# Narrower moving operands in the sums of squares, and more filler products at the head, in a one-layer decoder block

## Chip, cores and metric

The kernel runs on one core of a Trainium2 chip. The time is the device time of one execution in microseconds (us). A core has a matrix engine (TensorE, in the profile PE, its weight loads PEld), a vector engine (VectorE, DVE), an engine for activation functions (ScalarE, ACT), a general one (GpSimd, POOL) and queues for transfers (SP's queue carries nearly all of them here).

## What is computed

One layer over 512 tokens of 1024 features, all float32: two gated feed-forward parts with a token-mixing part between them, each behind an RMSNorm whose result is scaled and shifted by values from a conditioning vector; a last RMSNorm at the end.

```python
def rmsnorm(x, g):
    xf = x.astype(jnp.float32)
    y = xf * lax.rsqrt(jnp.mean(xf * xf, axis=-1, keepdims=True) + EPS)
    return (y * g.astype(jnp.float32)).astype(x.dtype)
...
def reference(x, c, positions, w_ada, b_ada, g_norm_ffn1, w_ffn1_in, ...):
    cos, sin = rope_tables(positions, x.dtype)
    cond = jax.nn.silu(c)
    h = x
    for l in range(DEPTH):
        mod = cond @ w_ada[l] + b_ada[l]
        sh1, sc1, gt1, sh2, sc2, gt2, sh3, sc3, gt3 = [
            m[:, None, :] for m in jnp.split(mod, N_MOD, axis=-1)]
        u = modulate(rmsnorm(h, g_norm_ffn1[l]), sh1, sc1)
        h = h + 0.5 * gt1 * swiglu(u, w_ffn1_in[l], w_ffn1_out[l])
        u = modulate(rmsnorm(h, g_norm_mix[l]), sh2, sc2)
        h = h + gt2 * token_mixing(u, cos, sin, w_in[l], ...)
        u = modulate(rmsnorm(h, g_norm_ffn2[l]), sh3, sc3)
        h = h + 0.5 * gt3 * swiglu(u, w_ffn2_in[l], w_ffn2_out[l])
    return rmsnorm(h, g_final)
```

What matters for the change is the mean of squares over the 1024 features, which every one of the four RMSNorms needs for each token.

## The kernel before

**Layout.** Features lie on the 128 partitions, tokens along the free dimension: the running state is eight tiles H[0] to H[7] of 128 features by 512 tokens. A sum over features is therefore a sum over partitions and over the eight tiles. The tiles' squares are first added up elementwise (on VectorE); the sum over the 128 partitions is then a matrix product. The stationary operand is a 128x128 piece of the squares (features by tokens), the moving operand a 128x128 tile of ones (`self.ones`), so that the output has tokens on partitions, with the same sum in each of its 128 columns. One column per piece is read (`bank[:, ::P]`) by the square root, whose result goes to `r4`: four columns, one for each 128 tokens. A reciprocal on VectorE follows. Then `spread` (line 460; in the head line 1678) makes from r4 a tile in which every partition has the factors of all tokens, by a product whose stationary operand is a column of r4 broadcast and whose moving operand is the identity.

**The stream.** The weights arrive by transfer on SP's queue, are split into a high part (line 317, ScalarE) and a low part (line 329, VectorE), and each product of the large matrices is three passes (lines 360 to 362, 747 to 749, and in the head 1718, 1720, 1722). Nothing reorders the work: each engine runs its instructions in the order in which the code writes them.

**Where the sums of squares are.** `stats_t` (line 442) is called five times in the middle of the stream and once at the end: in `out_tail` for the first half of the tokens and in `head` for the second half, both of them twice (before token mixing, before the second feed-forward part), in `out_end` for the first half, and for the second half when the last product is over. That last call sums three tiles (`acc`, `s6`, `s`) instead of one, and `s`, the square of the last tile, is ready last. Two filler products (line 625) and the spread stand behind it.

**The head.** `startup` (line 1617) begins with five filler products on ones (line 1630). Transfers bring H in four pieces. ScalarE's silu of the conditioning vector is spread over the partitions by two products of 512 columns (line 1649) and copied by VectorE (line 1652). Then the squares of H[0] to H[7] follow one by one on ScalarE (line 1662). Those of H[0] and H[1] are summed over partitions by themselves; from then on VectorE adds two neighbours (line 1666), and the function `part` (line 1655, its products on line 1657) adds the pair's sums into bank 7: four products for a pair. Behind the pairs (2,3) and (4,5) stands one filler product (line 1669, made by `warm`, line 1624), behind the last pair and the square root (line 1670) two (line 1671). VectorE meanwhile works through the conditioning's dot products (`ada_do`, line 387), between whose halves the reciprocal is put (line 1675). The spread (line 1678), five fillers (line 1679), the scaling of tile 0 (line 467 on VectorE, line 479 on ScalarE) and the first pass of the main products (line 1718) follow in this order. Fillers write bank 5 and are read by nobody.

Of the kernel before, what the change touches and what calls it, by code (L numbers as in the profile page):

```python
# [14 lines left out]
P = 128  # L15
T = 512
HT = 256
D = 1024
KT = 8
DFF = 2816  # L20
# [26 lines left out]
def _fmajor(w, cols):  # L47
    k = w.shape[0] // P
    return w[:, cols].reshape(k, P, len(cols)).transpose(1, 0, 2).reshape(P, -1)


def _tiles(*starts):
    return [np.arange(s, s + P) for s in starts]


def _blocks(w, c0, c1, j):

    rows = (w[:D // 2], w[D // 2:])
    return [np.concatenate([_fmajor(rows[i], x) for x in _tiles(c + j * P, c + j * P + P)], axis=1)
# [80 lines left out]
def chunk_widths():  # L140
    outs = [D] * (KT // 2 * (len(PARTS) - 1)) + [(FT - PARTS[-1][0]) * P] * KT
    f1 = [2 * FIRST * P] * KT + [D] * (2 * (FT - FIRST)), outs
    mix = [D] * 24 + [4 * P] * 2 + ([D] * 4 + [4 * P] * 2) * (KT // 2 - 1) + [D] * KT
    return f1, mix, ([D] * (2 * FT), outs)


class Kernel:
# [6 lines left out]
    def plan(self):  # L154
# [21 lines left out]
        def blocks(recs):  # L176
# [5 lines left out]
            for need, src, make in ((0, r11, None), (1, x0, (x0, r12, r11)), (2, x1, (x1, r22, x0)), (3, r21, None),  # L182
                                    (3, r12, (r12, r22, r12)), (3, r22, None), (3, x0, (x0, r21, x1))):
                for j, x in enumerate((r11, r12, r22, r21)):
                    if x == src or (make and x in make):
                        self.last[n + j] = len(self.order)
                self.order.append((D, n + need, src, make))

# [175 lines left out]
    def settle(self, bank, hi, uh):  # L364

        self.nc.tensor.matmul(bank[:, :HT - SHIFT], hi, uh[:, SHIFT:HT], start=True, stop=True, skip_group_check=True)

# [74 lines left out]
    def stats_t(self, bank, hs, parts=None, between=None):  # L442


        n = (hs.stop - hs.start) // P
        r, c = self.r4[:, hs.start // P:hs.stop // P], slice(hs.start, hs.stop, P)
        parts = parts or (self.acc[:, hs],)
        for j, x in enumerate(parts):
            for i in range(n):
                self.nc.tensor.matmul(bank[:, hs.start + i * P:hs.start + i * P + P], x[:, i * P:i * P + P], self.ones,  # L450
                                      start=i == j == 0, stop=j == len(parts) - 1, skip_group_check=True)
        self.nc.scalar.activation(r, bank[:, c], AF.Sqrt, bias=self.eps, scale=1.0 / D)
        if between:
            between()
        self.nc.vector.reciprocal(r, r)
# [20 lines left out]
    def norm_u(self, n, k, hs, t, rest=True):  # L476
# [5 lines left out]
        if n == 2 and hs.start:  # L482
            u = self.U4[1][k // 4]
            act(u[:, k % 4 * HT:(k % 4 + 1) * HT], t[:, hs], AF.Identity, bias=S, scale=1.0)

# [33 lines left out]
    def out_tail(self, ms, ksrc, gate, nxt, squares):  # L519
# [3 lines left out]
        tiles, starts, put = {}, {}, []  # L523
        A, Bh = slice(0, HT), slice(HT, T)
        step = None
        self.held = self.pos
        for h, hs in enumerate((A, Bh)):
            for m in ms:
# [12 lines left out]
                for i, (hi, lo, uh, ul) in enumerate(ks):  # L541
# [6 lines left out]
                    self.mm3(bank[:, hs], hi, lo, uh[:, hs], ul[:, hs], i == 0, i == len(ks) - 1)  # L548
                s = squares(m)[:, :HT]
                self.tail_step(m, hs, bank, gate, s)  # L550
# [13 lines left out]
    def out_end(self, ms, ksrc, gate):  # L564
# [3 lines left out]
        tiles = {}  # L568
        A, Bh = slice(0, HT), slice(HT, T)
        rA, rB = self.B[6], self.B[7]  # L570
# [12 lines left out]
        for h, hs in enumerate((A, Bh)):  # L583
            for m in ms:
# [9 lines left out]
                for i, (hi, lo, uh, ul) in enumerate(tiles[m]):  # L594
# [9 lines left out]
                    self.mm3(bank[:, hs], hi, lo, uh[:, hs], ul[:, hs], i == 0, i == n - 1)  # L604
                s = self.tp.tile([P, T], F32, name="ut")[:, :HT]
                self.tail_step(m, hs, bank, gate, s)
# [1010 lines left out]
    def startup(self):  # L1617
        nc, a = self.nc, self.a
        v, M = nc.vector, nc.tensor.matmul


        def warm(n, x):
            for _ in range(n):
                M(self.B[5][:, :P], self.ones, x[:, :P], start=True, stop=True)


        nc.scalar.dma_start(self.cond[0:1, :], a["c"])
        nc.scalar.preload_act_table(AF.Silu)
        v.memset(self.ones, 1.0)
        warm(5, self.ones)  # L1630

        row = self.X[0]
        v.memset(row, 0.0)
        v.memset(self.eps, EPS)
        v.memset(self.hpi, float(np.pi / 2))
        for k in range(0, KT, 2):
            two = slice(k * T, (k + 2) * T)
            nc.sync.dma_start(self.Hall[:, two], a["xT"][:, two])
        self.ada_fetch(0)
        nc.sync.dma_start(self.vecs, a["vecs"])  # L1640
        self.ada_fetch(8, 2)
        nc.sync.dma_start(self.cst, a["cst"][:, :163])
        self.fetch(0)
        self.ada_fetch(1)
        self.ada_fetch(9)
        self.fetch(1)
        nc.scalar.activation(row[0:1, :], self.cond[0:1, :], AF.Silu)
        for i in range(2):
            M(self.B[i], self.ones, row[:, i * T:(i + 1) * T], start=True, stop=True)
        nc.scalar.preload_act_table(AF.Sqrt)  # L1650
        for i in range(2):
            v.tensor_copy(self.cond[:, i * T:(i + 1) * T], self.B[i])


        def part(s, first, last):
            for n in range(4):
                M(self.B[7][:, n * P:(n + 1) * P], s[:, n * P:(n + 1) * P], self.ones, start=first and n == 0, stop=last,
                  skip_group_check=True)

        s = [self.acc, self.R] + [self.Xall[:, i * T:(i + 1) * T] for i in range(2, KT)]  # L1660
        for k in range(KT):
            nc.scalar.activation(s[k], self.H[k], AF.Square)
            if k < 2:
                part(s[k], not k, False)
            elif k % 2:
                v.tensor_tensor(s[k - 1], s[k - 1], s[k], op=OP.add)
                part(s[k - 1], False, k == KT - 1)
                if k + 1 < KT:
                    warm(1, self.H[k])
        nc.scalar.activation(self.r4, self.B[7][:, ::P], AF.Sqrt, bias=self.eps, scale=1.0 / D)  # L1670
        warm(2, self.H[7])

        g, b1 = self.g(0), self.vecs[:, 8:16]
        self.ada_do(0)
        self.ada_do(8, 2, lambda: v.reciprocal(self.r4, self.r4))

        for n in range(4):
            M(self.B[6][:, n * P:(n + 1) * P], self.r4[:, n:n + 1].to_broadcast([P, P]), self.ident, start=True, stop=True)
        warm(5, self.H[7])
        v.scalar_tensor_tensor(b1, b1, 1.0, g, op0=OP.add, op1=OP.mult)  # L1680
        self.ada_fin("shift", 0, 1)

        def scale(k):
            m = self.mod[:, 8 + k:9 + k]
            v.scalar_tensor_tensor(m, m, g[:, k:k + 1], b1[:, k:k + 1], op0=OP.mult, op1=OP.add)

        scale(0)
        banks = list(self.B)
        full = slice(0, T)
        self.Rn = {0: self.B[6]}  # L1690
        self.split_hi()
        t = self.norm_t(0, 0, full)
        self.norm_u(0, 0, full, t, rest=False)
        self.ada_do(1)
        self.norm_b(0, 0, full, t)
        self.split_lo()
        nc.scalar.activation(self.R, self.B[6], AF.Copy)
        self.Rn[0] = self.R
        self.norm_x(0, full, t)
        for k in range(KT):  # L1700
            if k + 1 < KT:
                if k:
                    self.ada_do(k + 1)
                self.ada_fin("shift", k + 1, k + 2)
                self.ada_do(9 + k)
                scale(k + 1)
                t = self.norm_t(0, k + 1, full)
            self.split(k + 1)
            if k + 1 < KT:
                self.norm_u(0, k + 1, full, t)  # L1710
                self.norm_b(0, k + 1, full, t)
            if k + 2 < KT:
                self.ada_fetch(k + 2)
                self.ada_fetch(10 + k)
            self.fetch(k + 2)
            w = self.take()
            for (hi, lo), b in zip(w, banks):
                M(b, hi, self.UH[k], start=k == 0, stop=False)  # L1718
            for (hi, lo), b in zip(w, banks):
                M(b, hi, self.UL[k], start=False, stop=False)  # L1720
            for (hi, lo), b in zip(w, banks):
                M(b, lo, self.UH[k], start=False, stop=k == KT - 1)  # L1722
        self.ada_next = self.ada_ahead = 16
        self.ada_stop = 24
        self.bg_fetch()
        adds, self.splits = self.u_steps(0)
        for f in adds:
            f()
        for j in range(FIRST):
            self.split(self.pos + j)  # L1730
            self.fetch()
            self.ffn_post(j, self.ffn_silu(j, banks[2 * j]), banks[2 * j + 1])
# [59 lines left out]
```

## Time and profile before

| | |
|---|---|
| three runs | 991.28, 990.26, 991.11 us; median 991.11 |
| the profiled execution | 990.14 us, of which the span from the first to the last instruction is 988.4 us |
| TensorE busy | 980.2 us, 99% of the span, 6688 multiplications |
| VectorE, ScalarE busy | 783.5 us, 475.2 us |
| sums of squares, line 450 | 32 instructions, 348.4 to 981.0 us |
| sums of squares in the head, line 1657 | 40 instructions, 6.0 to 11.6 us |
| fillers of the head, line 1624 | 28 instructions, 1.0 to 14.6 us |

A float32 product is two instructions on TensorE, each with its own weight load. A row of the view in order of time has the start, the stretch that it covers, the engine, the line, the operation, output<-inputs, the shape and the count, and in brackets the idle time ahead of it and what ended it. A shape such as 128*64 128x256 has the stationary operand first (128 rows by 64 columns) and the moving one behind it (128 partitions by 256 columns). A row of a line's instructions has their durations as minimum/median/maximum in ns. A row of a group has its busy time in us and, behind the comma, the mean of one in ns. A row of TensorE's waits has the total in us, how often, and the longest. A row by stretch has the length, the busy time of PE, PEld, DVE, ACT and POOL with their instruction counts, the granted clock of TensorE, the share of the transfer engines and GB/s.

### The profile page before, as it was taken

How to read it: one execution, taken by the hardware profiler on the slowest of the kernel's cores; microseconds unless marked ns; L12 is line 12 of the kernel's file. 1: busy time of each engine (PE TensorE's matmuls, PEld its weight loads, DVE VectorE, ACT ScalarE, POOL GpSimd, SP SyncE). 2: the span in 40 equal slices, each digit the busy share in tenths (PEclk: the TensorE clock that was granted, in tenths of full speed). 3: DMA queues.
4: the chain of work that ended last, by engine and by line, in shares of the span. 5: the costliest groups of instructions: out<-in, count | busy, mean ns of one | idle time of the engine just before them, and what ended most of it. 6: DMA issues, size and time to landing. Idle time of an engine off the chain costs nothing.

```text
span 988.4 us, 16359 instructions
## 1 busy us (share of the span) xinstructions
PE 980.2 (99%) x6688; PEld 892.8 (90%) x6688; DVE 783.5 (79%) x1089; ACT 475.2 (48%) x713; POOL 29.7 (3%) x31
## 2 busy tenths in 40 slices
PE   9999999999999999999999999999999999999997
PEld 7888998989999899788879998998899898998997
DVE  7989979889797677888879877768787777676764
ACT  6453643625435453446545553455355254352553
POOL 0000000000000000006200000000000000000002
PEclk9999999999999999999999999999999999999999
DMA  9856445464563416654233326513344134241312
GB/s 348 279 191 230 150 149 186 157 195 164 181 204 110 138 57 200 224 184 160 67 125 110 107 74 221 172 47 103 103 153 133 47 119 135 86 150 44 108 42 86
DMA packets 44876, 141.74 MB, mean 143 GB/s; under 512 B 6273, under 2 KB 9089, under 8 KB 44802
## 3 DMA queue, kind: packets, MB, share of 16 engines
q1 hardware_dynamic: 44224, 140.18, 43.7%
q8 instruction: 52, 0.85, 0.4%
q10 hardware_dynamic: 578, 0.53, 0.2%
q14 instruction: 22, 0.18, 0.1%
HBM read 135.29 MB, written 2.24 MB: 139 GB/s over the span
## 4 chain that ended last, share of the span: by engine, by line
PE 94%; DVE 2%; SPq 1%; DMA 1%; issue 1%; ACT 0%; POOL 0%; POOLq 0%; DVEq 0%; ACTq 0%
PE bank L360 15%; PE bank L361 15%; PE bank L362 15%; PE bank L748 13%; PE bank L747 13%; PE bank L749 13%; PE bank L1718 2%; PE bank L1722 1%; PE bank L1720 1%; SPq L1055 1%; PE bank L1101 1%; PE bank L1399 1%; PE bank L1152 1%; PE bank L1400 1%; PE bank L1401 1%
## 5 line engine op out<-in xcount | busy, mean ns | idle before, releaser
L329 DVE TENSOR_TENSOR wlo<-raw,whi 128x1024 fp32r<-128x1024 f32 (+4 forms) x162 | 170.4, 1064 | 52.5 <-ACT whi L317 52.2
L747 PE MATMUL bank<-UH,whi 128*128 128x256 f32 x640 | 176.7, 276 | 0.0
L748 PE MATMUL bank<-UL,whi 128*128 128x256 f32 x640 | 176.7, 276 | 0.0
L749 PE MATMUL bank<-UH,wlo 128*128 128x256 f32 x640 | 176.7, 276 | 0.0
L317 ACT ACTIVATE whi<-raw 128x1024 fp32r<-128x1024 f32 (+4 forms) x162 | 146.3, 921 | 58.6 <-DVE raw L261 55.1
L360 PE MATMUL bank<-HI,whi 128*128 128x512 f32 (+1 forms) x406 | 146.2, 360 | 0.0
L361 PE MATMUL bank<-HK,whi 128*128 128x512 f32 (+1 forms) x406 | 145.9, 359 | 0.0
L362 PE MATMUL bank<-HI,wlo 128*128 128x512 f32 (+1 forms) x406 | 145.8, 359 | 0.0
L329 DVE TENSOR_TENSOR wlo<-X,whi 128x1024 fp32r<-128x1024 f32 (+3 forms) x104 | 111.8, 1083 | 30.9 <-ACT whi L317 30.5
L747 PEld LDWEIGHTS bank<-UH,whi 128*128 128x128 f32 x640 | 120.1, 188 | 0.4
L748 PEld LDWEIGHTS bank<-UL,whi 128*128 128x128 f32 x640 | 120.2, 188 | 0.0
L749 PEld LDWEIGHTS bank<-UH,wlo 128*128 128x128 f32 x640 | 120.1, 188 | 0.0
L747 PE MATMUL bank<-SH,whi 128*128 128x256 f32 x408 | 112.6, 276 | 0.0
L748 PE MATMUL bank<-SL,whi 128*128 128x256 f32 x408 | 112.6, 276 | 0.0
L749 PE MATMUL bank<-SH,wlo 128*128 128x256 f32 x408 | 112.6, 276 | 0.0
L317 ACT ACTIVATE whi<-X 128x1024 fp32r<-128x1024 f32 (+3 forms) x104 | 95.7, 943 | 34.1 <-DVE X L261 33.4
L360 PE MATMUL bank<-UH,whi 128*128 128x512 f32 (+1 forms) x304 | 105.7, 348 | 0.0
L361 PE MATMUL bank<-UL,whi 128*128 128x512 f32 (+1 forms) x304 | 104.3, 343 | 0.1
L362 PE MATMUL bank<-UH,wlo 128*128 128x512 f32 (+1 forms) x304 | 104.1, 342 | 0.0
L362 PEld LDWEIGHTS bank<-HI,wlo 128*128 128x128 f32 x406 | 76.2, 188 | 11.7
L360 PEld LDWEIGHTS bank<-HI,whi 128*128 128x128 f32 x406 | 76.2, 188 | 11.5
L361 PEld LDWEIGHTS bank<-HK,whi 128*128 128x128 f32 x406 | 76.3, 188 | 11.3
(344 smaller groups left out, 1837.3 us busy)
## 6 DMA issues: line engine op xcount, KB each, us to landing
raw<-wmix SPq DMA_DIRECT2D x44, 512.0 KB, 3.8
raw<-wf1i SPq DMA_DIRECT2D x31, 512.0 KB, 4.9
raw<-wf2i SPq DMA_DIRECT2D x30, 512.0 KB, 3.7
ada<-wada SPq DMA_DIRECT2D x23, 512.0 KB, 5.6
AR<-wada SPq DMA_DIRECT2D x19, 512.0 KB, 4.5
X<-wf2i SPq DMA_DIRECT2D x14, 512.0 KB, 3.6
cs<-wada SPq DMA_DIRECT2D x12, 512.0 KB, 3.7
X<-wf1i SPq DMA_DIRECT2D x12, 512.0 KB, 4.3
```

Source lines behind the costliest of these rows:

```text
L317: self.nc.scalar.activation(self.hi[:, y], r[:, x], AF.Copy)
L329: self.nc.vector.tensor_tensor(self.lo[:, y], r[:, x], self.hi[:, y], op=OP.subtract)
L360: M(ps, hi, uh, start=start, stop=False)
L361: M(ps, hi, ul, start=False, stop=False)
L362: M(ps, lo, uh, start=False, stop=stop)
L747: M(o, hi, uh, start=start and p == 0 and k == 0, stop=False, skip_group_check=True)
L748: M(o, hi, ul, start=False, stop=False, skip_group_check=True)
L749: M(o, lo, uh, start=False, stop=k == 3, skip_group_check=True)
L1055: nc.sync.dma_start(w[32 * o:32 * o + 32], t[32 * i:32 * i + 32])
L1101: nc.tensor.matmul(S[:, o], q[:, toks], k[:, ks], start=True, stop=True, skip_group_check=True)
L1152: self.nc.tensor.matmul(self.bO[64 * h:64 * h + 64, P * hp:P * hp + P], x, pt[:, (2 * h + j) * P:(2 * h + j + 1) * P], start=j == first, s ...
L1718: M(b, hi, self.UH[k], start=k == 0, stop=False)
```

## The change

The moving operand of every sum of squares becomes 16 columns of ones instead of 128, and so does the output of each; the column that the square root reads is the first of them. In the head, the fillers behind the pairs (2,3) and (4,5) become three products instead of one, and those behind the square root four instead of two.

```diff
+NARROW = 16
...
         for j, x in enumerate(parts):
             for i in range(n):
-                self.nc.tensor.matmul(bank[:, hs.start + i * P:hs.start + i * P + P], x[:, i * P:i * P + P], self.ones,
+                t = hs.start + i * P
+                self.nc.tensor.matmul(bank[:, t:t + NARROW], x[:, i * P:i * P + P], self.ones[:, :NARROW],
                                       start=i == j == 0, stop=j == len(parts) - 1, skip_group_check=True)
...
         def part(s, first, last):
             for n in range(4):
-                M(self.B[7][:, n * P:(n + 1) * P], s[:, n * P:(n + 1) * P], self.ones, start=first and n == 0, stop=last,
-                  skip_group_check=True)
+                M(self.B[7][:, n * P:n * P + NARROW], s[:, n * P:(n + 1) * P], self.ones[:, :NARROW],
+                  start=first and n == 0, stop=last, skip_group_check=True)
...
                 if k + 1 < KT:
-                    warm(1, self.H[k])
+                    warm(3, self.H[k])
         nc.scalar.activation(self.r4, self.B[7][:, ::P], AF.Sqrt, bias=self.eps, scale=1.0 / D)
-        warm(2, self.H[7])
+        warm(4, self.H[7])
```

## The prediction

> **What bounds the kernel now.** I read the page first, then the list of TensorE's waits, then the two lines that the change touches, then the head in order of time.
>
> ```profile
> span 988.4 us, 16359 instructions
> PE 980.2 (99%) x6688; PEld 892.8 (90%) x6688; DVE 783.5 (79%) x1089; ACT 475.2 (48%) x713; POOL 29.7 (3%) x31
> ...
> PE 94%; DVE 2%; SPq 1%; DMA 1%; issue 1%; ACT 0%; POOL 0%; POOLq 0%; DVEq 0%; ACTq 0%
> ```
>
> TensorE is busy for 99% of the span and owns 94% of the chain that ended last. Its waits on other engines, over the whole run, are these five:
>
> ```profile
> PE bank L1624 <- DVE ones L1629: 1.1, 1, 1.1
> PE bank L1718 <- ACT UH L479: 0.5, 1, 0.5
> PE bank L460 <- DVE r L455: 0.3, 1, 0.3
> PE bank L1678 <- DVE r L1675: 0.2, 1, 0.2
> PE bank L450 <- ACT ut L517: 0.2, 1, 0.2
> ```
>
> Together 2.3 us. So a TensorE instruction saved in the stream is time saved, a late start of the main stream at line 1718 has hardly any later wait to hide in, and the change can matter in three places: the head, the five sums inside the stream, and the sum at the very end.
>
> **The price of a sum of 16 columns.** Each float32 product is two instruction pairs, a weight load and a multiplication.
>
> ```profile
> L450 PE MATMUL bank<-ones,AR x24: 270/274/275, 348.4 to 979.7; 128*128 128x128 f32 x24
> ```
>
> The change leaves the weights (128x128 squares) as they are and shortens only what moves past them. The question is which of the two sets the pace. Loads:
>
> ```profile
> L1187 PEld LDWEIGHTS bank<-cst,f x8: 85/88/90, 502.3 to 502.9; 128*8 128x8 f32 x8
> L1152 PEld LDWEIGHTS bank<-probT,v x120: 132/137/137, 405.3 to 494.6; 128*64 128x64 f32 x120
> L450 PEld LDWEIGHTS bank<-ones,AR x24: 187/191/192, 348.3 to 979.5; 128*128 128x128 f32 x24
> 9.44 0.19 PEld L1657 LDWEIGHTS bank<-ones,X 128*128 128x128 f32 x1
> 9.44 0.30 PEld L1657 LDWEIGHTS bank<-ones,X 128*128 128x128 f32 x2
> 470.53 0.97 PEld L1101 LDWEIGHTS bank<-k,q 64*128 64x128 f32 x16 [0.17 <-issue]
> 501.25 0.21 PEld L1245 LDWEIGHTS bank<-k,wpool 64*64 64x64 f32 x8 [0.35 <-issue]
> ```
>
> 8, 64 and 128 columns take 88, 137 and 191 ns: (191-88)/120 = 0.86 ns a column over a fixed part, so 128 columns keep the load path 110 ns. The two rows at 9.44 say the same: after a pause of TensorE the first load runs 0.19 us, two end after 0.30, so the second begins 0.30-0.19 = 0.11 us behind the first, before any multiplication could have held it back. Today's pace is 0.111 us a pair ((0.97-0.19)/7 in the rows of eight loads below). Load and multiplication therefore cost the same today, and shortening one leaves the other. **I take 0.111 us a pair: nothing saved in the stream.** The other end is the 16 loads at line 1101, (0.97-0.19)/15 = 0.052 us each; there they alternate between two halves of the array's rows, which these do not. Farther off, line 1245's eight loads go to different quarters, (0.21-0.13)/7 = 0.011 us, the 0.13 us being (by the slope above) what one of 64 columns takes. Full-height loads of 128 columns are nearest the first two rows. A dearer pair than today's I exclude: the load is unchanged and the multiplication shorter.
>
> What does get shorter is the end of the last multiplication:
>
> ```profile
> L747 PE MATMUL bank<-UH,whi 128*128 128x256 f32 x640 | 176.7, 276 | 0.0
> L361 PE MATMUL bank<-HK,whi 128*128 128x512 f32 x298 | 116.0, 389 | 0.0
> ```
>
> 256 more columns are 113 ns, 0.44 ns a column; a float32 row of 128 columns lasts as long as 256 of these (275 at most against 276), so 112 columns fewer end 112 x 0.88 = 0.10 us sooner.
>
> [...]
>
> **The head, step by step.** Lines 1657 (sums), 1624 (fillers), 1666 (adds of squares).
>
> ```profile
> 6.46 1.75 PEld L1657 LDWEIGHTS bank<-ones,AR 128*128 128x128 f32 x15 [0.24 <-issue]
> 8.13 0.97 PEld L1657 LDWEIGHTS bank<-ones,X 128*128 128x128 f32 x8
> 8.70 0.69 DVE L1666 TENSOR_TENSOR X<-X 128x512 f32<-128x512 f32 x1 [0.75 <-ACT X L1662]
> 9.03 0.30 PEld L1624 LDWEIGHTS bank<-H,ones 128*128 128x128 f32 x2
> 9.44 0.97 PEld L1657 LDWEIGHTS bank<-ones,X 128*128 128x128 f32 x8
> 9.98 0.69 DVE L1666 TENSOR_TENSOR X<-X 128x512 f32<-128x512 f32 x1 [0.59 <-ACT X L1662]
> 10.33 0.30 PEld L1624 LDWEIGHTS bank<-H,ones 128*128 128x128 f32 x2
> 10.73 0.97 PEld L1657 LDWEIGHTS bank<-ones,X 128*128 128x128 f32 x8
> 11.61 0.53 PEld L1624 LDWEIGHTS bank<-H,ones 128*128 128x128 f32 x4
> 11.92 0.26 ACT L1670 ACTIVATE r<-bank,eps 128x4 f32<-128x4 f32 x1 [1.98 <-PE bank L1657]
> 12.35 0.17 DVE L1675 RECIPROCAL r<-r 128x4 f32<-128x4 f32 x1
> 12.57 0.97 PEld L1678 LDWEIGHTS bank<-cst,r 128*128 128x128 f32 x8 [0.43 <-DVE r L1675]
> 15.33 2.11 PE L1718 MATMUL bank<-UH,whi 128*128 128x512 f32 x8 [0.48 <-ACT UH L479]
> 20.87 1.67 PEld L1718 LDWEIGHTS bank<-UH,whi 128*128 128x128 f32 x8 [0.24 <-ACT UH L479]
> ```
>
> Today the last two sums start when their adds end (8.70+0.69 = 9.39, then 9.44; 9.98+0.69 = 10.67, then 10.73), and the fillers fill most of the gaps, which leave 0.19, 0.18 and, ahead of line 1678, 0.52 us. The change puts four more pairs (0.44 us) into each. With 0.111 us a pair: sums at 8.13 to 9.02, six filler pairs to 9.69, sums to 10.58, six to 11.24, sums to 12.13 (11.61 today, 0.52 later), eight filler pairs to 13.02. The bank is complete 0.52-0.10 = 0.42 us later, so the root (line 1670) runs from 12.34 to 12.60. Today the reciprocal does not wait for it (12.18 to 12.35 is VectorE's own order); then it will, starts about 12.63, 0.28 us late, and behind it wait VectorE's second half of line 387, lines 390, 1680, 400 and 1685. Line 1678 could follow at 12.85, but the fillers ahead of it in TensorE's order hold it to 13.02: **0.45 us late**. Line 467 waits for its products, line 479 for that, and the main stream for line 479: from 15.33 to 15.78. The second round (20.87) waits for the same engines, behind the same delay, so nothing is won back there. Bounds: with a pair of 0.052 us the narrow sums end before their adds and the fillers fit in; the head is then no later, nor earlier, since the reciprocal keeps its place in VectorE's order. Thus 0 to +0.45; I take +0.45.
>
> **The stream and the end.** Five calls of line 450 (two in out_tail, two in head, one in out_end) have four pairs each, 20 pairs at an unchanged 0.111: 0. Bounds: at 0.052, 20 x 0.059 = 1.2 us saved.
>
> ```profile
> 980.10 0.42 ACT L517 ACTIVATE ut<-H 128x256 f32<-128x256 f32 x1 [0.46 <-DVE H L516]
> 980.56 0.52 PEld L450 LDWEIGHTS bank<-ones,ut 128*128 128x128 f32 x4 [0.38 <-ACT ut L517]
> 981.31 0.26 ACT L452 ACTIVATE r<-bank,eps 128x2 f32<-128x2 f32 x1 [0.80 <-PE bank L450]
> 981.83 0.97 PEld L460 LDWEIGHTS bank<-cst,r 128*128 128x128 f32 x8 [0.30 <-DVE r L455]
> ```
>
> At the end only the four pairs behind the last square (980.10+0.42) are exposed; the eight ahead of them lie in that wait. The last multiplication ends 0.10 us sooner, the root, the reciprocal, line 460 and the stores follow: -0.10. At 0.052 a pair, three steps more, -0.18: -0.28.
>
> **Sum:** +0.45 + 0 - 0.10 = +0.35 us. The profiled execution took 990.14 us around its span of 988.4; the median of the three runs, 991.11, is 0.97 above it, and their spread is 1.02 us. The profile would be 990.5, the median **991.5 us**.
>
> **Rivals.** One: *half price*. Narrow loads overlap as at line 1101: 0 - 1.2 - 0.28 = -1.5 us, 989.6. For it: that row. Against it: its two row halves, and the two loads at 9.44.
>
> Two, the other side: *the clock falls in the head*.
>
> ```profile
> L1624 PE MATMUL bank<-ones x10: 421/421/579, 1.1 to 3.1; 128*128 128x128 f32 x10
> 6.03 0.59 PE L1649 MATMUL bank<-X,ones 128*128 128x512 f32 x1
> 984.50:985.00 0.50, 0.00 (x0) 0.00 (x0) 0.15 (x1) 0.00 (x0) 0.39 (x1) 1.00 1.01 338
> 985.00:986.00 1.00, 0.00 (x0) 0.00 (x0) 0.00 (x0) 0.00 (x0) 0.00 (x0) 0.63 1.01 339
> ```
>
> TensorE starts slow: 421 ns for what later takes 275. By 6.03 it is fast (512 columns in 0.59 us, more work than those 421 ns). So it took up to 5.0 us from the first product at 1.05. At the other end the granted clock (the third number from the end) is 1.00 to 985 and means 0.63 in the next microsecond, so it halves at 985.26. The last products ran from 981.83 to about 983.0: 1.2 of the last 3.4 us, 34%, did not hold it. After the change, if only moving columns count, the stretch from 6.46 to 9.69 holds 24 narrow pairs of 16 x 0.88 = 14 ns and six fillers of 0.11: 1.0 of 3.2 us, 31%. That is the point: below about 34% by moving columns the clock would halve near 9.7. Up to 5.0 us at half speed lose 2.5 us of products, with the +0.35 a total of +2.9: 994.0. Against it: if loads count as work, the stretch is full. The end's case also had 2.3 us of complete silence. [...]
>
> Three: *the loads hide entirely*, 0.011 us a pair as at line 1245: 20 x 0.10 + 3 x 0.10 + 0.10 = -2.4 us, 988.7. Against it stands everything at 128 full columns.
>
> Four: *the head's delay is swallowed* by a later wait, leaving -0.10, 991.0. The five waits leave 0.5 us for it at most, and those at 1718 come before or with the delay.
>
> **How the numbers follow.** My forecast 0.52; half price 0.14; clock 0.21; hidden loads 0.05; swallowed 0.08. A measurement of this kernel can tell about 0.2%, 2.0 us, from no change. Beyond that lie rival two above and rival three below; from half price (1.5 us) a little falls outside with the runs' 1 us spread, and from the forecast as little above. Faster 0.08, same 0.69, slower 0.23. The range goes from half price less some spread, 989.4, to the clock's 994.0; outside it lie most of rival three and about half of rival two.
>
> **What would show it.** Right: line 1657 and 450 loads still 0.11 us apart, their multiplications about 0.18 us long; line 1675 near 12.6, line 1678 near 13.0, line 1718 near 15.8; the last root near 0.10 us sooner behind the last square. Wrong: pairs of 0.06 us or less; fillers at line 1624 after 9 us lasting 421 ns; line 1718 still at 15.3.

## The result and the profile after

| | kernel before | changed kernel |
|---|---|---|
| runs | 22, median 990.32 us (989.95 to 991.28) | 22, median 995.05 us (990.25 to 995.72) |
| profiled execution | 990.14 us, span 988.4 | 995.06 us, span 993.3 |
| ratio | | 1.0033, 95% interval 1.0022 to 1.0044 |

The change made the kernel slower. The ratio, 0.33%, is an average over two sorts of runs: of the 22, fifteen took 994.68 to 995.72 us and seven 990.25 to 990.88, with nothing between them. The runs of before form one group. So the usual loss is 995.05 - 990.32 = 4.7 us, and in a third of the runs there is none. The granted clock of the whole execution tells the same two sorts apart: it is 0.993 to 0.995 in each of the fifteen, and 0.998 to 1.000 in each of the seven, as in the runs of the kernel before.

The profile of the changed kernel is one of the fifteen. Its page, the lines that answer to those of before:

```profile
span 993.3 us, 16383 instructions
...
PE 985.6 (99%) x6700; PEld 898.8 (90%) x6700; DVE 783.4 (79%) x1089; ACT 474.9 (48%) x713; POOL 29.7 (3%) x31
...
PEclk7999999999999999999999999999999999999999
...
PE 95%; DVE 2%; SPq 1%; issue 1%; ACT 1%; POOL 0%; DMA 0%; POOLq 0%; ACTq 0%; DVEq 0%
```

Twelve more instruction pairs, as the added fillers give; every other engine as before; and a first slice of TensorE's clock at 7 tenths, where the kernel before has 9. The same by stretch (length, busy time of PE, PEld, DVE, ACT and POOL with counts, the granted clock, the transfers' share, GB/s):

```profile
6.02:9.43 3.41, 3.41 (x27) 2.96 (x26) 2.38 (x4) 2.81 (x6) 0.00 (x0) 1.00 1.01 393
9.43:19.67 10.24, 10.24 (x49) 10.24 (x49) 4.59 (x15) 1.94 (x6) 0.00 (x0) 0.50 1.02 369
...
19.67:22.00 2.33, 2.31 (x14) 1.86 (x13) 2.33 (x5) 2.33 (x4) 0.00 (x0) 1.00 0.66 193
```

The clock was halved for 10.24 us, beginning 3.41 us after it had first become full at 6.02. (That moment is the first entry of the clock in the trace. Ahead of it the rows by stretch print 1.00 all the same, but the products of line 1627 last 421 ns there and their loads 333 ns, as in the stretch that has 0.50; at 1.00 it is 274 and 192 ns.) TensorE was busy all the while, for 10.24 of 10.24 us, with pairs that stand 0.21 us apart instead of 0.111 (worked out below the rows). In order of time (line numbers are three higher than before):

```profile
6.66 1.75 PEld L1660 LDWEIGHTS bank<-ones,AR 128*128 128x128 f32 x15 [0.24 <-issue]
8.33 0.97 PEld L1660 LDWEIGHTS bank<-ones,X 128*128 128x128 f32 x8
9.22 1.20 PEld L1627 LDWEIGHTS bank<-H,ones 128*128 128x128 f32 x6
10.30 1.83 PEld L1660 LDWEIGHTS bank<-ones,X 128*128 128x128 f32 x8
12.01 1.40 PEld L1627 LDWEIGHTS bank<-H,ones 128*128 128x128 f32 x6
13.29 1.83 PEld L1660 LDWEIGHTS bank<-ones,X 128*128 128x128 f32 x8
15.00 1.83 PEld L1627 LDWEIGHTS bank<-H,ones 128*128 128x128 f32 x8
15.26 0.26 ACT L1673 ACTIVATE r<-bank,eps 128x4 f32<-128x4 f32 x1 [5.22 <-PE bank L1660]
16.70 1.83 PEld L1681 LDWEIGHTS bank<-cst,r 128*128 128x128 f32 x8
18.41 1.80 PEld L1627 LDWEIGHTS bank<-H,ones 128*128 128x128 f32 x10
20.42 2.11 PE L1721 MATMUL bank<-UH,whi 128*128 128x512 f32 x8
```

Eight loads take 0.97 us at 8.33 and 1.83 us from 10.30 on: (1.83-0.33)/7 = 0.21 us a pair, 0.33 us being one load there, instead of 0.111. The main stream starts at 20.42 where it started at 15.33, 5.09 us later, and the execution took 4.92 us longer (995.06 - 990.14): almost nothing wins it back. What the 5.09 us consist of is worked out below.

And the end. The square of the last tile is complete at 985.10+0.42 = 985.52, the root starts 0.70 us behind it; before, it was 981.31 - 980.52 = 0.79.

```profile
985.10 0.42 ACT L520 ACTIVATE ut<-H 128x256 f32<-128x256 f32 x1 [0.47 <-DVE H L519]
985.56 0.52 PEld L453 LDWEIGHTS bank<-ones,ut 128*128 128x128 f32 x4 [0.38 <-ACT ut L520]
986.22 0.26 ACT L455 ACTIVATE r<-bank,eps 128x2 f32<-128x2 f32 x1 [0.71 <-PE bank L453]
```

### The profile page after: what moved, and what is told of

The parts are those of the page before. It is cut to its first block, busy times and chain, and to the rows that moved or that the text cites. A ratio compares the mean times of both kernels' runs of the same rounds, so it can differ in the third digit from the quotient of the medians.

```text
span 993.3 us, 16383 instructions
## 1 busy us (share of the span) xinstructions
PE 985.6 (99%) x6700; PEld 898.8 (90%) x6700; DVE 783.4 (79%) x1089; ACT 474.9 (48%) x713; POOL 29.7 (3%) x31
## 4 chain that ended last, share of the span: by engine, by line
PE 95%; DVE 2%; SPq 1%; issue 1%; ACT 1%; POOL 0%; DMA 0%; POOLq 0%; ACTq 0%; DVEq 0%
PE bank L362 15%; PE bank L363 15%; PE bank L364 15%; PE bank L752 13%; PE bank L750 13%; PE bank L751 13%; PE bank L1721 1%; PE bank L1725 1%; PE bank L1723 1%; SPq L1058 1%; PE bank L1402 1%; PE bank L1104 1%; PE bank L1155 1%; PE bank L1403 1%; PE bank L1404 1%
```

## The experiments

The kernel before ran beside each; the three sets of it have medians of 990.38, 990.33 and 990.31 us. Each row of a table below is a median (lowest to highest) over eleven or twelve runs, and the ratio's 95% interval. Edits are shown against the changed kernel, with `...` where lines are left out.

### Which part of the change it is

**Narrow sums in the stream and at the end only:**

```diff
-                M(self.B[7][:, n * P:n * P + NARROW], s[:, n * P:(n + 1) * P], self.ones[:, :NARROW],
-                  start=first and n == 0, stop=last, skip_group_check=True)
+                M(self.B[7][:, n * P:(n + 1) * P], s[:, n * P:(n + 1) * P], self.ones, start=first and n == 0, stop=last,
+                  skip_group_check=True)
...
-                    warm(3, self.H[k])
+                    warm(1, self.H[k])
...
-        warm(4, self.H[7])
+        warm(2, self.H[7])
```

> Narrow sums in the stream and at the end only; the head as before. Theory A (TensorE's clock falls in the head because few columns move there; the narrow sums elsewhere cost nothing and end 0.1 us sooner): the clock stays, all runs within 0.5 us of the kernel before, median 0.1 us under it. Theory B (the added fillers are the cost): the same. Theory C (narrow sums cost wherever they stand): slower, by up to 5 us, in some runs or in all.

**Narrow sums and added fillers in the head only:**

```diff
-                t = hs.start + i * P
-                self.nc.tensor.matmul(bank[:, t:t + NARROW], x[:, i * P:i * P + P], self.ones[:, :NARROW],
+                self.nc.tensor.matmul(bank[:, hs.start + i * P:hs.start + i * P + P], x[:, i * P:i * P + P], self.ones,
```

> Narrow sums and added fillers in the head; wide sums in the stream and at the end. A: two groups of runs, about two in three at 995 and the rest at 990.4. B: the same. C: part of the 4.7 us only.

**The added fillers only** (both edits of the sums undone, `warm(3)` and `warm(4)` kept):

> All sums wide as before, the added fillers stay. A: the clock stays, one group of runs, later than before by what the fillers take in TensorE's order, +0.45 us: line 1718's work starts near 15.8 us. B: near 995, since the fillers are the cost. The clock by theory A needs narrow sums.

**Narrow sums in the head without the added fillers** (the second edit above, and `warm(1)`, `warm(2)` as before):

> Narrow sums in the head, fillers as before, wide sums elsewhere. A: fewer columns move (24 narrow pairs and one filler product instead of three between 6.5 and 9.7 us), so the clock falls at least as often as with the added fillers, in two of three runs or more, to 994 to 996 us; a fall is the cheaper by the missing fillers at half speed, 0.2 us a product. B: no loss, about 990.3, in all runs.

| | median us | lowest to highest | ratio, interval |
|---|---|---|---|
| stream and end only | 990.03 | 989.67 to 991.09 | 0.9998, 0.9989 to 1.0007 |
| head only | 995.13 | 990.32 to 995.32 (8 of 12 over 995) | 1.0032, 1.0019 to 1.0045 |
| fillers only | 990.83 | 990.47 to 991.50 | 1.0006, 0.9997 to 1.0014 |
| head, no added fillers | 992.60 | 990.95 to 993.32 | 1.0021, 1.0012 to 1.0030 |

The whole loss is in the head, and it needs the narrow sums. With the fillers alone the granted clock is 0.998 to 1.000 in all eleven runs. They are not the one group that I expected, though: six took 990.47 to 990.83 us and five 991.38 to 991.50, so the median, 0.45 us over the kernel before, stands at the edge of a gap, and its interval reaches to no difference. The profile measures the fillers better:

```profile
16.06 2.14 PE L1720 MATMUL bank<-UH,whi 128*128 128x512 f32 x8 [0.48 <-ACT UH L481]
```

The main stream starts at 16.06 us, where I expected 15.8. In this execution the clock became full at 6.13, in the profile of the kernel before at 5.63. Half a microsecond more at half clock costs 0.25 us, an estimate that the copy behind the products of 512 columns bears out (6.91 against 6.66). That leaves 15.81 against 15.33: the fillers delay the head by 0.48 us.

The narrow sums without the added fillers let the clock fall in the profiled execution too, and no run was under 990.95. I had expected 994 to 996; the median was 992.60, and in the profile the fall lasted 6.82 us. So theory B falls, and C with it. The third and the second kernel have the same TensorE instructions, in the same order with the same loads, in the head; only the number of columns that move differs. What the added fillers do is mixed: with them a third of the runs escape, and a fall costs about twice as much (995.13 against 992.60, over a kernel before at 990.38).

```profile
7.32:10.74 3.42, 3.42 (x33) 3.42 (x31) 2.69 (x5) 2.31 (x5) 0.00 (x0) 1.00 1.04 391
10.74:17.56 6.82, 6.82 (x33) 6.82 (x33) 4.09 (x13) 1.72 (x4) 0.00 (x0) 0.50 1.04 405
```

These stretches are of the kernel without the added fillers: full from 7.32, fallen 3.42 us later, for 6.82 us. In the four profiles with a fall that are shown by stretch here its length is a whole multiple of 3.41 us: 10.24, 6.82, 3.42 and 10.24.

### How many columns hold the clock

**64 columns in the head's sums, the rest as changed:**

```diff
-                M(self.B[7][:, n * P:n * P + NARROW], s[:, n * P:(n + 1) * P], self.ones[:, :NARROW],
+                M(self.B[7][:, n * P:n * P + 64], s[:, n * P:(n + 1) * P], self.ones[:, :64],
```

> The changed kernel with 64 columns instead of 16 in the head's sums. Theory A (what holds the clock is the share of time in which columns move, over a stretch of 3.4 us): between 6.0 and 9.4 us the share goes from 34% (the changed kernel, where the clock fell) to 64%, and in no stretch is it under 50%; if the point lies between 34 and 60%, the clock stays in all runs and what is left is the fillers' delay: 990.8, one group. Theory D (any product narrower than 128 columns lets it fall, or what falls has to do with the bank's columns that are left unwritten): two groups again, 995 and 990.4.

**32 columns** (the same edit with 32):

> 32 columns in the head's sums. A: the share between 6.0 and 9.4 us is about 44%, inside the band that is open (34% fell). If the clock falls in some runs, in fewer than with 16 columns (15 of 22); if in none, the point lies between 34 and 44%. D: as often as with 16.

**64 columns, fillers as before** (the edit above with `warm(1)` and `warm(2)`):

> 64 columns in the head's sums, fillers as before, 16 columns in the stream and at the end. A: the share stays over 50% in every stretch of 3.4 us (59% where 16 columns had 22%), so the clock stays, the head is on time, and the end is 0.1 us sooner: 990.2. If the point lies near 60%, falls come back here first, as 992 to 993. D: falls as with 16 columns and no added fillers, all runs over 990.9.

**32 columns, fillers as before:**

> 32 columns in the head's sums, fillers as before, 16 columns in the stream and at the end. Theory A (the share of 3.4 us in which columns move; 34% fell, 44% held): the share depends on where the stretch begins; from 7.3 us, where the run without added fillers and with 16 columns had 22%, 32 columns make 34%; so the clock falls in some of the runs, to 992 to 993, and holds in others, 990.3. Theory E (16 columns are too few in themselves, whatever the share; 32 are enough): no run falls, 990.3.

**16 columns in the first 16 pairs alone, fillers as before:**

```diff
+                w = NARROW if s is self.acc or s is self.R else P
-                M(self.B[7][:, n * P:n * P + NARROW], s[:, n * P:(n + 1) * P], self.ones[:, :NARROW],
+                M(self.B[7][:, n * P:n * P + w], s[:, n * P:(n + 1) * P], self.ones[:, :w],
```

> 16 columns in the head's sums of H[0] and H[1] alone (16 pairs), 128 columns in the other three; fillers as before; 16 columns in the stream and at the end. A: the narrow stretch lasts 1.8 us, so every 3.4 us hold at least about 50%: the clock stays, 990.2. E: it falls as with 16 columns everywhere, in two of three runs or more.

| | median us | lowest to highest | ratio, interval |
|---|---|---|---|
| 64 columns, added fillers | 990.66 | 990.25 to 991.38 | 1.0004, 0.9995 to 1.0013 |
| 32 columns, added fillers | 990.70 | 990.28 to 991.49 | 1.0005, 0.9996 to 1.0015 |
| 64 columns, fillers as before | 990.32 | 990.02 to 991.69 | 1.0001, 0.9992 to 1.0009 |
| 32 columns, fillers as before | 991.54 | 990.96 to 993.15 | 1.0014, 1.0005 to 1.0023 |
| 16 columns in 16 pairs, fillers as before | 990.41 | 990.04 to 990.84 | 0.9999, 0.9990 to 1.0008 |

Thirty-two columns hold in eleven runs with the added fillers and fail without them; sixteen columns hold where only the first pairs have them. So neither the width by itself (E) nor narrowness as such (D) decides. In the second row the five slowest runs, 990.90 to 991.49, have a granted clock of 0.999, which leaves no room for a fall of 3.41 us (half of it is 0.0017 of the span). My expectation for the fourth row was too kind: I had some runs hold, and none was under 990.96. The granted clock is 0.998 in the six runs up to 991.54 and 0.995 to 0.996 in the five above. The profile is one of the six (991.02), and the clock fell in it; that it fell in the other five is likely by their times and not shown. The clock became full early, at 5.32, and survived the first window; the second took it:

```profile
5.32:8.73 3.41, 3.27 (x23) 2.55 (x21) 2.08 (x3) 3.16 (x6) 0.00 (x0) 1.00 1.02 415
8.73:12.14 3.41, 3.41 (x29) 3.22 (x29) 2.69 (x5) 1.38 (x4) 0.00 (x0) 1.00 1.07 378
12.14:15.56 3.42, 3.38 (x17) 3.09 (x16) 2.33 (x11) 1.39 (x3) 0.00 (x0) 0.50 1.03 410
15.56:18.97 3.41, 3.34 (x18) 2.73 (x18) 3.41 (x8) 2.78 (x4) 0.00 (x0) 1.00 1.03 410
```

The loads in the second window of this kernel, from which its share of moving columns can be counted by hand:

```profile
8.54 0.75 PEld L1660 LDWEIGHTS bank<-ones,X 128*128 128x128 f32 x6
9.21 0.30 PEld L1627 LDWEIGHTS bank<-H,ones 128*128 128x128 f32 x2
9.60 0.97 PEld L1660 LDWEIGHTS bank<-ones,X 128*128 128x128 f32 x8
10.48 0.30 PEld L1627 LDWEIGHTS bank<-H,ones 128*128 128x128 f32 x2
10.89 0.97 PEld L1660 LDWEIGHTS bank<-ones,X 128*128 128x128 f32 x8
11.78 0.63 PEld L1627 LDWEIGHTS bank<-H,ones 128*128 128x128 f32 x4
```

From 8.73 to 12.14 there are about 20 sums of 32 x 0.88 = 28 ns and seven fillers of 0.11 us: 0.56 + 0.77 = 1.3 of 3.41 us, 38%. Counted so over the multiplications of each trace (columns times 0.44 ns, twice for float32, twice again at half clock, one behind the other; good to some 0.06), the window with the smallest share of each of these traces gives the table. The kernel that we just saw stands there twice, as its two windows had different outcomes.

| kernel, window in us | share with columns moving | clock behind it |
|---|---|---|
| 16 columns, no added fillers, 7.32 to 10.74 | 0.18 | falls |
| changed kernel, 6.02 to 9.43 | 0.30 | falls |
| head only, 6.62 to 10.03 | 0.31 | falls |
| changed kernel once more (below), 6.97 to 10.38 | 0.31 | falls |
| 32 columns, fillers as before, 8.73 to 12.14 | 0.38 | falls |
| 32 columns, added fillers, 6.04 to 9.45 | 0.41 | stays |
| 64 columns, fillers as before, 8.81 to 12.22 | 0.45 | stays |
| 32 columns, fillers as before, 5.32 to 8.73 | 0.45 | stays |
| 16 columns in 16 pairs, 5.75 to 9.17 | 0.54 | stays |
| 64 columns, added fillers, 6.51 to 9.93 | 0.61 | stays |

The order by share is the order by outcome. Columns placed otherwise within the records (at their starts or 0.08 us behind, at 0.42 or 0.44 ns each) move single shares by up to 0.06. In each such count the highest of the falling windows (0.34 to 0.37) stays below the lowest of the others (0.40 to 0.46). The expectations above rest on such a count, 0.03 to 0.04 higher for the same windows. The cleanest pair is the changed kernel and the one with 32 columns, whose windows begin within 0.02 us of each other and differ in the width alone:

```profile
6.04:9.45 3.41, 3.41 (x27) 2.98 (x26) 2.45 (x4) 2.96 (x7) 0.00 (x0) 1.00 1.01 387
9.45:12.86 3.41, 3.41 (x32) 3.41 (x32) 2.45 (x5) 0.81 (x4) 0.00 (x0) 1.00 1.07 393
```

The loads are busy for 2.98 us of it where the changed kernel's were for 2.96; its clock stays at 1.00, the other's went to 0.50. So loads alone, busy for 2.96 of 3.41 us, did not hold the clock. With the width of the moving operand go the columns that are written to the bank and the multiplications that are done; these runs cannot tell the three apart.

At half clock the counts say which windows brought it back. In the changed kernel the windows from 9.43 and from 12.85 have a share of 0.57 each and do not raise the clock; the third, from 16.26, has nothing but products of 128 columns (1.00) and does. In the second profile of the changed kernel, below, 0.52 and 0.62 did not. With narrow sums in the stream and at the end only, a window ahead of the first rise, 0.81 to 4.22, has about 0.78, and the clock did not rise behind it. Of the windows counted, those with 0.85 or more all raised it.

**The changed kernel once more:**

> The changed kernel once more, for a profile. A: if the clock falls, its fall lies one or two windows of 3.41 us behind the moment it became full, and it lasts three of them; if it does not, the moment it became full lies well ahead of 6.0 us, and the main stream starts 0.3 to 0.5 us later than before for the same moment.

It took 995.27 us, with the clock full at 6.97, fallen one window later, for three windows:

```profile
6.97:10.38 3.41, 3.41 (x31) 3.25 (x30) 2.68 (x5) 2.45 (x5) 0.00 (x0) 1.00 1.03 391
10.38:20.62 10.24, 10.24 (x51) 10.24 (x50) 4.63 (x13) 2.23 (x5) 0.00 (x0) 0.50 0.98 366
20.62:24.00 3.38, 3.38 (x17) 2.79 (x17) 3.34 (x9) 1.84 (x3) 0.00 (x0) 1.00 0.53 166
```

An execution that escapes was not caught in a profile. That its clock does not fall is shown by its granted clock (0.998 to 1.000). That it is one whose clock becomes full early is argued from where its windows would then lie, not shown.

### Towards a kernel that beats both

**The stream and the end narrow, a second time:**

> The kernel of the first run (narrow sums in the stream and at the end, the head as before) a second time, to see 0.1 us better: A: 0.1 to 0.3 us under the kernel before. No difference would say that the sooner end of the last sum is lost in the stores.

**Wide sums in the head with no filler between them, narrow elsewhere** (the first kernel above, and):

```diff
-                if k + 1 < KT:
-                    warm(1, self.H[k])
```

> Sums of 128 columns in the head with no filler between them (two products, four pairs, fewer than before), 16 columns in the stream and at the end. A: the wide sums hold the clock alone (over 80% of each 3.4 us), and where it becomes full late the head has 0.2 to 0.4 us less in TensorE's order: median 0.1 to 0.4 us under the kernel before, 990.0 to 990.2, the slowest runs nearer to 990.5 than to 991. If fillers were needed between the sums: falls, 992 or more.

| | median us | lowest to highest | ratio, interval |
|---|---|---|---|
| stream and end only, again | 990.25 | 989.88 to 990.54 | 0.9998, 0.9989 to 1.0007 |
| no fillers between wide sums | 990.07 | 989.64 to 991.62 | 0.9998, 0.9989 to 1.0007 |

Both beat the changed kernel. Against the kernel before, the medians are 0.1 to 0.35 us lower in three tries out of three, with intervals that include no difference: a gain of 0.1 us at the end fits, and is not shown by the times. No run shows that the fillers between wide sums are needed: ten of the eleven runs end by 990.51, and the one at 991.62 is within what the kernel before showed (991.77).

## Why the prediction was right or wrong

**The price of a narrow pair: right.** The loads still stand 0.111 us apart (0.97 us for eight at 8.33; 0.53 us for the four at 353.33, a call in the stream, shown below), and the narrow sums in the stream gave no gain that eleven runs can tell. Half price and hidden loads, rivals one and three, are out.

**The end: right,** 0.09 us for 0.10. But I had read the multiplication's record wrongly. The changed kernel's narrow sums at full clock, by line, between that call's loads and the fillers of the head:

```profile
353.33 0.53 PEld L453 LDWEIGHTS bank<-ones,AR 128*128 128x128 f32 x4
L1660 PE MATMUL bank<-ones,AR x16: 179/262/263, 6.7 to 8.2; 128*128 128x16 f32 x16
L1627 PE MATMUL bank<-H,ones x30: 274/421/561, 9.3 to 20.1; 128*128 128x128 f32 x30
```

Most narrow sums show 262 ns, not about 180: the start stands in the record before the load is through (the second multiplication of the call starts at 353.47, its load ends at 353.64), and only the root's start shows the sooner end.

**The head's delay by the fillers: right in size** where the clock stays: 0.48 us in the profile with the fillers alone, worked out above. The medians, 0.45 us over with the fillers alone and 0.33 and 0.37 with 64 and 32 columns, where the end is 0.1 us sooner, fit this with wide intervals. Of the changed kernel's loss it is a small part.

**The base and the runs that do not fall.** The forecast of 991.5 stood on a median of three runs, 991.11, which lies 0.79 us above that of 22. On 990.32 its +0.35 would give 990.7 and rival two's +2.9 would give 993.2. The seven runs that do not fall have a median of 990.33, so the +0.35 is not seen in them either. If they are the ones whose clock becomes full early, that could be the reason; no profile shows it.

**The likeliest case: wrong in two runs of three.** What happened there is rival two. The step that failed is the sentence by which I set it behind: "if loads count as work, the stretch is full". They did not hold the clock: equal loads (2.96 and 2.98 of 3.41 us), 16 columns against 32, and the clock fell or stayed. So the forecast had the clock's part in its sum at nothing. The sign of being wrong that I had named is there, too: the fillers after 9 us last 421 ns at the median (line 1627 above). The case that mattered thus stood in the text, and I gave it 0.21.

That its two shares fit the measured ones is luck. The 34% counts the whole 1.2 us from the first load to the end of the last record; the eight multiplications in it move columns for 8 x 0.112 = 0.90 of 3.41 us, 26%, and the head's 31% would not have lain under that. The 31%, close to the 30% of the trace, was counted from 6.46 to 9.69 with six fillers; the window that decided, 6.02 to 9.43, has the last products of 512 columns in it, until about 6.8, and hardly a filler.

**The price of the fall: mis-sized.** The term was "Up to 5.0 us at half speed lose 2.5 us", taken from how long the clock needs to rise at the start of the program. The clock was at half for 10.24 us, and the main stream lost 4.41 us by it. That is read from the kernel with 32 columns, whose clock became full within 0.02 us of the changed kernel's and did not fall (its row first):

```profile
16.01 1.69 PEld L1721 LDWEIGHTS bank<-UH,whi 128*128 128x128 f32 x8 [0.67 <-ACT UH L482]
20.42 0.76 PEld L1721 LDWEIGHTS bank<-UH,whi 128*128 128x128 f32 x4 [0.21 <-ACT UH L482]
```

So the 5.09 us are 20.42 - 16.01 = 4.41 of the fall, 0.48 of the fillers, and 0.20, an estimate (half of the delay, as above), because the clock became full 0.39 us later than in the profile of the kernel before. Half of 10.24 us would be 5.12; of the 0.71 that the main stream did not lose, 0.46 lie in the shorter wait of the two rows, and the rest is open.

Why it lasted so long: at the start TensorE has only wide products in its way. After the fall it had the narrow sums still ahead of it, which then took 0.21 us a pair, and with the six filler pairs between two of them a window came to a share of 0.57. That did not raise the halved clock, where shares of 0.54 and 0.61 held a full one (the table above). The total was 4.7 us where rival two had 2.9; the median of 995.05 lies above the range's 994.0.

**Swallowed delay: not seen.** Of the main stream's 5.09 us, the run kept 4.92; the end gave 0.09 back, and less than 0.1 us is left over.

## What to carry to other kernels

The narrow sums saved nothing at an unchanged 0.111 us a pair, and in the head they let TensorE's clock fall in fifteen runs of 22: before narrowing what moves past a full load, count the share of every 3.41 us in which columns move (here the clock fell at 0.38 and less and stayed at 0.41 and more). Fillers are not free insurance: here they had to bring that share up before the clock fell, for afterwards they cost 0.21 us a pair instead of 0.111. And where the median and the lowest run lie far apart with nothing between, look at the clock by stretch before you look at any engine's busy time.

## What was not expected of the hardware

TensorE's clock was halved while its multiplications were busy without a gap by the profile (3.41 of 3.41 us) and its loads nearly so (2.96). By the counts above and the lengths of the stretches it changed by windows of 3.41 us: falls at shares of moving columns of 0.18 to 0.38, none at 0.41 and more; rises at 0.85 and more, none at 0.78 and less. Its changes stand on one grid from the head to the end. In the kernel before the clock rises at 5.629 us and falls, after the last product, at 985.254, 287 windows of 3.4133 us (a third of the 10.24) later; in the changed kernel the last rise, at 19.674, and the fall at 992.473 are 285 windows apart. Between the shares of fall and rise it stayed what it was: full at 0.41 to 0.61, halved at 0.52 to 0.78. So a head with a share of 0.57 was held at half speed by its own slowness.

The moment of the rise differs from run to run: the clock became full between 4.53 and 7.64 us in the fourteen profiles. The execution with 7.64 (wide sums in the head) took 991.09 us, the slowest of its eleven; but the one with 4.53, of the same kernel, took 990.54, also the slowest of its eleven, so the moment by itself does not set the time.
